# Moving the turned copy, the stores, the square sums and the weight preparation within a hand-ordered seven-product kernel

## Chip, cores, metric

One core of one Trainium2 chip. The metric is the device time of one execution in microseconds; lower is better.

## What is computed

A trunk of one layer over 2048 tokens of width 1024, all in float32:

```python
h = _rmsnorm(x, norm_w[layer])
proj = h @ w_in[layer]                       # split among four branches
y_a = _conv_mixer(a_h, a_b, a_c, a_z, ...)   # causal depthwise convolution, gated
y_b = _gla_mixer(g_q, g_k, g_v, g_lr, g_z, ...)   # gated linear attention, state per chunk of 64
y_c = _pool_mixer(p_u, p_z, ...)             # causal window means of 2, 4, 8, 16
y_d = _ssd_mixer(s_xbc, s_dt, s_z, ...)      # state space branch, state per chunk of 64
mix = jnp.concatenate([y_a, y_b, y_c, y_d], axis=-1)
x = x + mix @ w_out[layer]
return _rmsnorm(x, final_norm_w)
```

## The kernel before

**Arithmetic.** Every large float32 product is made of three matmuls on rounded halves: `split` (lines 172 to 174) casts a tile to `hi` on ACT (ScalarE) and takes `lo = raw - hi` on DVE (VectorE). `mm12` (lines 235 to 241) is one product of a 128x512 weight tile and a 512x512 quarter of the activations: four k-slices times three matmuls, 12 matmuls of 128x512.

**Seven products.** A 2x2 block product is done with seven `mm12` instead of eight, by sums and differences of quarters. `first7` (line 245) makes a11 x b11 in an accumulator `a`. `pair7` (lines 251 to 280) makes the other six. In order on TensorE they are s2, a12, s1, s3, then, through `after`, the first product (a11) of the next pair, then a22 and s4. The pair opens with the turned copy b = -a, an ACT instruction from PSUM to PSUM (lines 253 to 255); s2 accumulates onto b. There are four accumulator banks (`ps_acc`): a, b, e, and the a of the next pair. After each product a consumer empties a bank: `cp2` after s2, `ev11` after a12, `cp3` and a subtraction of e after s3, `ev21` after a22, and a last subtraction `d12 = e - d12` after s4.

**Runs.** The text calls one such product with its consumer and the `tick()` behind it a run: a pair has seven ticks. `tick` (lines 190 to 198) takes one step of four generators (`chunks`, the recurrence over chunks; `prep_`, the weights of the next pair; `side`, activations of the next stage, twice) and then runs those entries of `queue` that `later(n, fn)` put off by n ticks.

**Weights.** `prep7` (lines 216 to 233) asks for four raw 128x512 tiles, loads them, and then gives one step a tick: split a11 with the three POOL (GpSimd) sums s1, s2 and s3; split a12; and so on to s4. Its first step, the loads, is taken by `next(prep_[0])` ahead of the pair. It is drained at the end of each pair. The pool `pw` has 18 such tiles.

**Fixed order.** `strict[0]` turns on an order written out by hand: each engine's instructions, and the DMA issues on SP (SyncE), are issued in the order in which the program's text made them (class `Ordered`, lines 60 to 79). An instruction that waits holds up everything behind it on its engine. It is on from the first pair of each segment.

**Stages.** The tokens come in two segments of 1024. A segment begins with token-major blocks whose order the compiler picks; then come ten pairs in the fixed order, `qk, B, xs, C, a_h, a_c, a_b, a_z, p_u, p_z` (line 41). The recurrence (`chunk_loop`, lines 450 to 514) starts in pair C and ends near a_b; its output runs through `gate_outputs` and `to_mix` to DRAM (`yd`). Pairs a_z and p_z write `yd` by `spill` (line 578). In the last two pairs of a segment `side` makes the next segment's activations or, in the second, the halves of w_out. Then come eight row pairs (lines 1091 to 1106), each two tiles of 128 rows of `yd` times w_out: `Rows` (lines 1052 to 1089) adds the residual x, `square` (line 1025) sums the squares on ACT, `emit` (line 1032) does the inverse root on DVE in small steps (`rsqrt`, line 154), scales two halves of a row tile and stores them (`out`). `load_rows` reads `yd`, `load_x` reads x.

**The fold.** In the first segment `fold_pu` (line 346) multiplies the pool branch's weights on TensorE and writes them to DRAM (`wd`), before the pairs begin.

Of the kernel before, what the change touches and what calls it, by code (L numbers as in the profile page):

```python
# [55 lines left out]
def tile_hybrid_trunk(ctx: ExitStack, tc: tile.TileContext, xtok, xT, wkv, wch, wpu, wz, wo, pw_, nw, par, gw, fnw, out):  # L56
# [150 lines left out]


# [7 lines left out]
    def prep7(load, w7):  # L216

        a11, a12, a21, a22 = [wt("wr", F32) for _ in range(4)]
        load(a11, a12, a21, a22)
        yield 1  # L220
        w7['a11'] = split_w(a11)
        s1 = wt("ws", F32)
        pool.tensor_add(s1, a21, a22)
        s2 = wt("ws", F32)
        pool.tensor_add(s2, s1, a11)
        pool.tensor_add(a21, a21, a11)
        yield 1
        w7['a12'] = split_w(a12)
        pool.tensor_add(a12, a12, s2)
        yield 1  # L230
        for n, r in (('s2', s2), ('s1', s1), ('s3', a21), ('a22', a22), ('s4', a12)):
            w7[n] = split_w(r)
            yield 1
# [11 lines left out]
    def first7(w7, H):  # L245

        a = acc()
        mm12(a, w7['a11'], H['b11'], True)
        ahead[0] = a

    def pair7(w7, H, ev11, ev21, d12, d22, cp2, cp3, done, after=None):

        a = ahead[0]
        b = acc()
        act.activation(b, a, AF.Copy, scale=-1.0)
# [17 lines left out]
        mm12(b, w7['a22'], H['t4'], False)  # L273
        ev21(b)
# [71 lines left out]
    def fold_pu(j):  # L346

        mix = gen("mix")[:, :P]
        sp.dma_start(mix, pw_[j])

        def fold(h):
            wu = gen("wu")[:, :512]
            sp.dma_start(wu, wpu[j][:, h * 512:(h + 1) * 512])
            tp = tr()
            for i in range(4):
                pe.matmul(tp[:, i * P:(i + 1) * P], lhsT=wu[:, i * P:(i + 1) * P], rhs=mix, start=True, stop=True)
            raw = gen("fw")[:, :512]
            act.copy(raw, tp)
            sp.dma_start(wd[j][:, h * 512:(h + 1) * 512], raw)
        later(2, lambda: fold(0))  # L360
        later(3, lambda: fold(1))
# [88 lines left out]
    def chunk_loop(kv, kt, q, aG, aD, bt, xs, wt_, cc, after):  # L450
# [53 lines left out]
        for tt in range(TT):  # L504
            if tt:
                outputs(tt - 1, st)
            yield 1
# [5 lines left out]
        yield 1  # L513
        outputs(TT - 1, st)

    def gate_outputs(s, f, kv, xs, rt):
# [38 lines left out]
        def to_mix(tt):  # L555
# [11 lines left out]
            sp.dma_start(yd[s * TT + tt, :, 2:4, :], y3[:, 0:2, :])  # L567
            sp.dma_start(yd[s * TT + tt, :, 6:8, :], y3[:, 2:4, :])
# [9 lines left out]
    def spill(s, f, blk, y):  # L578

        t0 = s * TT + f * 4  # L580
        sp.dma_start(yd[t0:t0 + 4, :, blk, :].rearrange("t p n -> p t n"), y.rearrange("p (t n) -> p t n", t=4))
# [315 lines left out]
    for s in range(NSEG):  # L897
# [42 lines left out]
        prep_[0] = prep7(load_pair(PAIRS[0]), w7)  # L940
# [11 lines left out]
        drain(prep_)  # L952
        std.clear()
# [37 lines left out]
        first7(w7, H)  # L991
        for n, name in enumerate(PAIRS):
            w_next, wk = {}, []
            if n + 1 < len(PAIRS):
                prep_[0] = prep7(load_pair(PAIRS[n + 1]), w_next)
            elif s + 1 < NSEG:
                prep_[0] = kv_gen(wk)
            else:
                prep_[0] = prep7(load_rows(0), w_next)
            if w_next is not None and not (n + 1 == len(PAIRS) and s + 1 < NSEG):  # L1000
                next(prep_[0])
# [11 lines left out]
            drain(prep_)  # L1013
            w7 = w_next
        drain(side)
        strict[0] = s + 1 == NSEG
# [15 lines left out]
    def emit(tt, r, sq):  # L1032
        rs = rsqrt(None, None, 1, v=sq[:, 3:4])
        for c in range(2):
            cs = slice(c * 512, (c + 1) * 512)
            vec.scalar_tensor_tensor(r[:, cs], r[:, cs], rs, fw[c], ALU.mult, ALU.mult)
            sp.dma_start(out[tt, :, cs], r[:, cs])
# [14 lines left out]
    class Rows:  # L1052
# [12 lines left out]
        def ev11(self, o):  # L1065
            vec.tensor_tensor(self.r[0][0], o, self.x[0][0], ALU.add)
            square(self.r[0][0], self.x[0][0], self.sq[0], 0)

        def ev21(self, o):
            vec.tensor_tensor(self.r[1][0], o, self.x[1][0], ALU.add)  # L1070
            square(self.r[1][0], self.x[1][0], self.sq[1], 1)
# [7 lines left out]
        def done(self, j):  # L1079
            if j == 0:  # L1080
                square(self.r[1][1], self.x[1][1], self.sq[1], 0)
            elif j == 1:
                later(2, lambda: emit(self.tt + 1, self.rows[1], self.sq[1]))
            else:
                square(self.r[0][1], self.x[0][1], self.sq[0], 1)
                if self.tt + 2 < NTT:
                    later(3, lambda: emit(self.tt, self.rows[0], self.sq[0]))
                else:
                    emit(self.tt, self.rows[0], self.sq[0])

    rows = Rows(0)
    for tt in range(0, NTT, 2):
        w_next = {}
        nxt = []
        if tt + 2 < NTT:
            prep_[0] = prep7(load_rows(tt + 2), w_next)
            next(prep_[0])
# [4 lines left out]
        drain(prep_)  # L1102
# [83 lines left out]
```

## Time and profile before

| | us |
|---|---|
| median of 2 runs | 1009.86 (1004.94 to 1014.78) |
| the profiled execution | 1012.62 |
| its span, first to last instruction | 1010.8 |
| mean granted TensorE clock | 0.909 |

Times in the trace are microseconds from the span's start. Busy PE time counts overlapping matmuls once. A number in square brackets behind an instruction is the time that its engine idled just before it, and what ended that idle time. Every instruction of the fixed order has line 76, the line of the wrapper, so instructions are told apart by their tiles: `wh` and `wl` are the halves of weights, `wr` raw weights, `ws` the sums, `hh` and `hl` the halves of activations, `acc` the accumulators, `r` rows of the result, `xk` rows of x.

### The profile page before, as it was taken

To read this page: it belongs to the slowest core of one execution; us is meant where nothing else is said; L and a number is where in the kernel's file an instruction comes from. 1 tells how busy PE (TensorE), PEld (TensorE's weight loads), DVE (VectorE), ACT (ScalarE), POOL (GpSimd) and SP (SyncE) were. 2 spreads that over 40 slices of the span, in tenths; PEclk is the share of its full clock that TensorE was granted. 3 is DMA by queue.
4 is the path that set the end of the run, shared out by engine and by line. 5 is a ranking of instruction groups with operands and counts; after the bars stand their busy time and mean duration, and the time that the engine had idled before them with its cause. 6 is when DMAs were issued, how large, how long until landed. Compare 5 with 4: busy or idle time off the path is not lost. (4 is left out here: it accounts for less than half of the span.)

```text
span 1010.8 us, 11513 instructions
## 1 busy us (share of the span) xinstructions
PE 824.1 (82%) x3944; PEld 656.8 (65%) x3944; DVE 679.4 (67%) x1252; ACT 402.9 (40%) x804; POOL 257.1 (25%) x206
## 2 busy tenths in 40 slices
PE   7996798888868978899988889598862877787775
PEld 5885676666646757887766667477751666576564
DVE  5779556675857689835257766867699456655665
ACT  6756544442335334453344523334533222222221
POOL 0018222143421122302221445122243222220120
PEclk7999799999979999899999989889986988988888
DMA  9416411111113441222211102112701433233321
GB/s 321 150 59 204 159 42 42 42 42 49 36 52 115 148 158 47 79 74 81 86 42 42 42 1 84 53 53 88 287 21 37 150 125 108 92 114 125 117 92 63
DMA packets 57579, 94.09 MB, mean 93 GB/s; under 512 B 5840, under 2 KB 20656, under 8 KB 57008
## 3 DMA queue, kind: packets, MB, share of 16 engines
q1 hardware_dynamic: 57520, 93.35, 28.0%
q8 instruction: 31, 0.51, 0.2%
q14 instruction: 28, 0.23, 0.1%
HBM read 71.31 MB, written 22.02 MB: 92 GB/s over the span
## 5 line engine op out<-in xcount | busy, mean ns | idle before, releaser
L76 PE MATMUL acc<-hl,wh 128*128 128x512 f32 x782 | 335.8, 429 | 118.9 <-ACT acc L76 76.7
L76 PE MATMUL acc<-hh,wl 128*128 128x512 f32 x784 | 324.5, 414 | 8.1 <-DVE wl L76 8.1
L76 PE MATMUL acc<-hh,wh 128*128 128x512 f32 x784 | 324.5, 414 | 0.0
L76 PEld LDWEIGHTS acc<-hl,wh 128*128 128x128 f32 x782 | 159.0, 203 | 168.7 <-ACT acc L76 84.5
L76 PEld LDWEIGHTS acc<-hh,wl 128*128 128x128 f32 x784 | 158.6, 202 | 45.2 <-DVE wl L76 8.5
L76 PEld LDWEIGHTS acc<-hh,wh 128*128 128x128 f32 x784 | 159.8, 204 | 31.7
L76 DVE TENSOR_TENSOR wl<-wr,wh 128x512 fp32r<-128x512 f32 (+1 forms) x136 | 102.9, 757 | 82.0 <-ACT wh L76 74.5
L76 POOL TENSOR_TENSOR ws<-wr,wr 128x512 f32<-128x512 f32 x24 | 33.9, 1411 | 372.9 <-PE acc L76 121.6
L76 ACT CAST wh<-wr 128x512 fp32r<-128x512 f32 (+1 forms) x138 | 82.7, 604 | 62.4 <-DMA wr<-yd 53.1
L71 PE MATMUL acc<-wl,hh 128*128 128x512 f32 (+1 forms) x224 | 80.7, 364 | 8.2 <-DVE wl L76 7.4
L71 PE MATMUL acc<-wh,hl 128*128 128x512 f32 (+1 forms) x224 | 79.0, 358 | 0.0
L76 DVE SCALAR_TENSOR_TENSOR t<-xin,prm,t 128x512 f32<-128x512 f32 x72 | 59.4, 825 | 28.8 <-ACT t L76 25.9
L71 PE MATMUL acc<-wh,hh 128*128 128x512 f32 (+1 forms) x224 | 74.0, 363 | 4.8 <-ACT wh L71 4.8
L76 ACT ACTIVATE xk<-r 128x512 f32<-128x512 f32 x32 | 20.2, 631 | 96.6 <-DVE r L76 96.6
L71 PEld LDWEIGHTS acc<-wl,hh 128*128 128x128 f32 x224 | 44.7, 200 | 14.8 <-DVE wl L76 8.2
L76 POOL TENSOR_TENSOR wr<-wr,ws 128x512 f32<-128x512 f32 x26 | 37.1, 1425 | 65.6 <-DVE wl L76 45.8
L76 DVE TENSOR_TENSOR wl<-ws,wh 128x512 fp32r<-128x512 f32 x52 | 44.6, 857 | 8.7 <-ACT wh L76 5.5
L71 PEld LDWEIGHTS acc<-wh,hh 128*128 128x128 f32 x224 | 41.9, 197 | 11.4 <-ACT wh L71 6.7
L71 PEld LDWEIGHTS acc<-wh,hl 128*128 128x128 f32 x224 | 44.6, 200 | 4.9
L71 DVE TENSOR_TENSOR hl<-xq,hh 128x1024 fp32r<-128x1024 f32 (+1 forms) x36 | 44.1, 1245 | 4.3 <-ACT hh L71 4.3
L71 POOL TENSOR_TENSOR xq<-xq,xq 128x1024 f32<-128x1024 f32 x8 | 25.9, 3256 | 70.8 <-DVE xq L71 41.4
L71 ACT CAST hh<-xq 128x1024 fp32r<-128x1024 f32 (+1 forms) x36 | 35.1, 996 | 16.8 <-DVE xq L71 16.7
(216 smaller groups left out, 1153.0 us busy)
## 6 DMA issues: line engine op xcount, KB each, us to landing
wr<-in_wch SPq DMA_DIRECT2D x72, 256.0 KB, 2.9
xk<-in_xtok SPq DMA_DIRECT2D x64, 256.0 KB, 5.2
wr<-yd SPq DMA_DIRECT2D x32, 256.0 KB, 4.0
out<-r SPq DMA_DIRECT2D x32, 256.0 KB, 2.1
xq<-in_xT SPq DMA_DIRECT2D x14, 512.0 KB, 6.4
wr<-in_wz SPq DMA_DIRECT2D x16, 256.0 KB, 2.7
szd<-z SPq DMA_DIRECT2D x16, 256.0 KB, 2.8
sz<-szd SPq DMA_DIRECT2D x16, 256.0 KB, 2.9
```

What stands on the lines that cost most here:

```text
L71: return f(*args, **kw)
L76: r = f(*args, **kw)
```

## The change

It keeps the fixed order, and edits what stands where in it.

1. **The turned copy** moves out of the start of `pair7` into `second7`, which is called inside the pair before, behind the a22 product and ahead of `ev21`. The first pair of a segment calls it straight after `first7`.
2. **Weight preparation.** `load7` issues the loads where the pair starts, as before; `prep7` then makes one quarter a tick, and is not drained at the end of a pair. Steps left over are chained in front of the next pair's. The first pair of a segment waits one tick more (`n = 1`), so a11 of the next pair is split in tick 2 of a pair where it was tick 1, and s4 in tick 1 of the pair that uses it. s4 is summed into the tile of s2, after the split of s2, where it was summed into a12.
3. **Stores.** `store` puts a DMA issue off by one tick: the `y` and `yd` stores and the `out` stores of `emit`.
4. **Square sums** of the row pairs are put off by one tick, which puts them behind that tick's preparation step; the last `emit` as well.
5. **The recurrence** gives its two `yield`s after `advance`, so `outputs` of one step comes two ticks after `advance`, with `update` of the next step right behind it in the same tick. It needs 17 ticks where it needed 18.
6. **The fold** loads both halves of `wu` at once where `fold_pu` is called, and multiplies a tick later. The queue is emptied before the fixed order begins.

```diff
--- before.py
+++ after.py
@@ -205,19 +205,27 @@
         for _ in g or ():
             pass
-    def prep7(load, w7):
-        a11, a12, a21, a22 = [wt("wr", F32) for _ in range(4)]
-        load(a11, a12, a21, a22)
-        yield 1
+    def store(dst, src):
+        later(1, lambda: sp.dma_start(dst, src))
+    def load7(load):
+        raw = [wt("wr", F32) for _ in range(4)]
+        load(*raw)
+        return raw
+    def prep7(raw, w7, n=0):
+        a11, a12, a21, a22 = raw
+        for _ in range(n):
+            yield 1
         w7['a11'] = split_w(a11)
         s1 = wt("ws", F32)
         pool.tensor_add(s1, a21, a22)
@@ -226,9 +234,11 @@
         pool.tensor_add(a21, a21, a11)
         yield 1
         w7['a12'] = split_w(a12)
-        pool.tensor_add(a12, a12, s2)
         yield 1
-        for n, r in (('s2', s2), ('s1', s1), ('s3', a21), ('a22', a22), ('s4', a12)):
+        w7['s2'] = split_w(s2)
+        pool.tensor_add(s2, s2, a12)
+        yield 1
+        for n, r in (('s1', s1), ('s3', a21), ('a22', a22), ('s4', s2)):
             w7[n] = split_w(r)
             yield 1
@@ -246,13 +256,17 @@
         a = acc()
         mm12(a, w7['a11'], H['b11'], True)
-        ahead[0] = a
+        ahead[0] = [a, None]
+    def second7():
+        b = acc()
+        act.activation(b, ahead[0][0], AF.Copy, scale=-1.0)
+        ahead[0][1] = b
     def pair7(w7, H, ev11, ev21, d12, d22, cp2, cp3, done, after=None):
-        a = ahead[0]
-        b = acc()
-        act.activation(b, a, AF.Copy, scale=-1.0)
+        a, b = ahead[0]
         mm12(b, w7['s2'], H['t2'], False)
         cp2(d12, b)
         tick()
@@ -271,6 +285,8 @@
             after()
             tick()
         mm12(b, w7['a22'], H['t4'], False)
+        if after is not None:
+            second7()
         ev21(b)
         done(1)
         tick()
@@ -349,16 +365,19 @@
         sp.dma_start(mix, pw_[j])
         def fold(h):
-            wu = gen("wu")[:, :512]
-            sp.dma_start(wu, wpu[j][:, h * 512:(h + 1) * 512])
+            wu = wus[h]
             tp = tr()
             for i in range(4):
                 pe.matmul(tp[:, i * P:(i + 1) * P], lhsT=wu[:, i * P:(i + 1) * P], rhs=mix, start=True, stop=True)
             raw = gen("fw")[:, :512]
             act.copy(raw, tp)
             sp.dma_start(wd[j][:, h * 512:(h + 1) * 512], raw)
-        later(2, lambda: fold(0))
-        later(3, lambda: fold(1))
+        wus = []
+        for h in range(2):
+            wus.append(gen("wu")[:, :512])
+            sp.dma_start(wus[h], wpu[j][:, h * 512:(h + 1) * 512])
+        later(3, lambda: fold(0))
+        later(4, lambda: fold(1))
     last_exp = [None]
@@ -504,13 +523,12 @@
         for tt in range(TT):
             if tt:
                 outputs(tt - 1, st)
-            yield 1
             ups = update(tt, wx)
             if tt + 1 < TT:
                 wx = inputs(tt + 1)
             st = [advance(tt, i, ups[i]) for i in range(2)]
             yield 1
-        yield 1
+            yield 1
         outputs(TT - 1, st)
     def gate_outputs(s, f, kv, xs, rt):
@@ -564,8 +582,8 @@
                 act.activation(y[:, (2 + b) * P:(3 + b) * P], tp[:, (2 + b) * P:(3 + b) * P], AF.Copy,
                                scale=pcol('snw', b))
             y3 = y.rearrange("p (b n) -> p b n", b=4)
-            sp.dma_start(yd[s * TT + tt, :, 2:4, :], y3[:, 0:2, :])
-            sp.dma_start(yd[s * TT + tt, :, 6:8, :], y3[:, 2:4, :])
+            store(yd[s * TT + tt, :, 2:4, :], y3[:, 0:2, :])
+            store(yd[s * TT + tt, :, 6:8, :], y3[:, 2:4, :])
         later(3, scales_)
         for i, tt in enumerate(ts4):
@@ -578,7 +596,7 @@
     def spill(s, f, blk, y):
         t0 = s * TT + f * 4
-        sp.dma_start(yd[t0:t0 + 4, :, blk, :].rearrange("t p n -> p t n"), y.rearrange("p (t n) -> p t n", t=4))
+        store(yd[t0:t0 + 4, :, blk, :].rearrange("t p n -> p t n"), y.rearrange("p (t n) -> p t n", t=4))
     QS = ((0, 0), (0, 1), (1, 0), (1, 1))
@@ -937,7 +955,7 @@
             block_tok([std[0, 0], std[0, 1]], tt, wzt, o)
             spill_z(tt, o)
         w7 = {}
-        prep_[0] = prep7(load_pair(PAIRS[0]), w7)
+        prep_[0] = prep7(load7(load_pair(PAIRS[0])), w7)
         if s + 1 < NSEG:
             fold_pu(0)
             later(3, lambda: fold_pu(1))
@@ -950,6 +968,8 @@
             spill_z(4 + i, o[i])
         drain(side)
         drain(prep_)
+        while queue:
+            tick()
         std.clear()
         raws.clear()
         strict[0] = True
@@ -989,16 +1009,16 @@
             return a_pair(s, name)
         first7(w7, H)
+        second7()
         for n, name in enumerate(PAIRS):
             w_next, wk = {}, []
+            left = prep_[0] or ()
             if n + 1 < len(PAIRS):
-                prep_[0] = prep7(load_pair(PAIRS[n + 1]), w_next)
+                prep_[0] = chain(left, prep7(load7(load_pair(PAIRS[n + 1])), w_next, 0 if left else 1))
             elif s + 1 < NSEG:
-                prep_[0] = kv_gen(wk)
+                prep_[0] = chain(left, kv_gen(wk))
             else:
-                prep_[0] = prep7(load_rows(0), w_next)
-            if w_next is not None and not (n + 1 == len(PAIRS) and s + 1 < NSEG):
-                next(prep_[0])
+                prep_[0] = chain(left, prep7(load7(load_rows(0)), w_next))
             if name == 'C':
                 later(3, lambda: chunks.__setitem__(0, chunk_loop(kv, kt, q, aG, aD, bt, xs, wt_, cc, after_chunks)))
             if name == 'a_z':
@@ -1010,9 +1030,10 @@
             def after():
                 first7(w_next, H if n + 1 < len(PAIRS) else Hw)
             pair7(w7, H, *consumers(name), after=after if n + 1 < len(PAIRS) or s + 1 == NSEG else None)
-            drain(prep_)
             w7 = w_next
         drain(side)
+        if s + 1 < NSEG:
+            drain(prep_)
         strict[0] = s + 1 == NSEG
@@ -1034,7 +1055,7 @@
         for c in range(2):
             cs = slice(c * 512, (c + 1) * 512)
             vec.scalar_tensor_tensor(r[:, cs], r[:, cs], rs, fw[c], ALU.mult, ALU.mult)
-            sp.dma_start(out[tt, :, cs], r[:, cs])
+            store(out[tt, :, cs], r[:, cs])
     def load_x(tt):
         xk = []
@@ -1064,11 +1085,11 @@
         def ev11(self, o):
             vec.tensor_tensor(self.r[0][0], o, self.x[0][0], ALU.add)
-            square(self.r[0][0], self.x[0][0], self.sq[0], 0)
+            later(1, lambda: square(self.r[0][0], self.x[0][0], self.sq[0], 0))
         def ev21(self, o):
             vec.tensor_tensor(self.r[1][0], o, self.x[1][0], ALU.add)
-            square(self.r[1][0], self.x[1][0], self.sq[1], 1)
+            later(1, lambda: square(self.r[1][0], self.x[1][0], self.sq[1], 1))
         def cp2(self, d, o):
             vec.scalar_tensor_tensor(d, o, 1.0, self.x[0][1], ALU.mult, ALU.subtract)
@@ -1078,28 +1099,26 @@
         def done(self, j):
             if j == 0:
-                square(self.r[1][1], self.x[1][1], self.sq[1], 0)
+                later(1, lambda: square(self.r[1][1], self.x[1][1], self.sq[1], 0))
             elif j == 1:
                 later(2, lambda: emit(self.tt + 1, self.rows[1], self.sq[1]))
             else:
-                square(self.r[0][1], self.x[0][1], self.sq[0], 1)
+                later(1, lambda: square(self.r[0][1], self.x[0][1], self.sq[0], 1))
                 if self.tt + 2 < NTT:
                     later(3, lambda: emit(self.tt, self.rows[0], self.sq[0]))
                 else:
-                    emit(self.tt, self.rows[0], self.sq[0])
+                    later(1, lambda: emit(self.tt, self.rows[0], self.sq[0]))
     rows = Rows(0)
     for tt in range(0, NTT, 2):
         w_next = {}
         nxt = []
         if tt + 2 < NTT:
-            prep_[0] = prep7(load_rows(tt + 2), w_next)
-            next(prep_[0])
+            prep_[0] = chain(prep_[0] or (), prep7(load7(load_rows(tt + 2)), w_next))
             later(3, lambda: nxt.append(Rows(tt + 2)))
         rows.take()
         pair7(w7, H, rows.ev11, rows.ev21, rows.r[0][1], rows.r[1][1], rows.cp2, rows.cp3, rows.done,
               after=(lambda: first7(w_next, H)) if tt + 2 < NTT else None)
-        drain(prep_)
         w7 = w_next
         rows = nxt[0] if nxt else None
     while queue:
```

## Rows read from the trace of the kernel before

**Rows 1.** The page's busy time by engine.
```profile
PE 824.1 (82%) x3944; PEld 656.8 (65%) x3944; DVE 679.4 (67%) x1252; ACT 402.9 (40%) x804; POOL 257.1 (25%) x206
```

**Rows 2.** TensorE's waits: sum in us, how many, the longest.
```profile
PE acc L76 <- ACT acc L76: 76.7, 22, 8.7
PE acc L76 <- DVE r L76: 25.2, 8, 5.2
PE oy L76 <- POOL sb L76: 14.7, 12, 2.6
PE tr L71 <- DMA wu<-in_wpu: 12.4, 1, 12.4
```

**Rows 3.** Windows: length, busy PE, PEld, DVE, ACT, POOL, clock, DMA, GB/s.
```profile
115.70:377.90 262.20, 221.01 (x1133) 172.12 (x1134) 174.64 (x333) 104.02 (x210) 75.42 (x68) 0.93 0.23 73
...
480.40:710.70 230.30, 196.82 (x1024) 152.96 (x1024) 149.78 (x292) 94.26 (x190) 69.14 (x64) 0.93 0.18 55
710.70:782.20 71.50, 44.67 (x176) 35.60 (x176) 61.53 (x60) 29.43 (x46) 26.27 (x12) 0.81 0.32 113
...
807.60:980.50 172.90, 134.68 (x504) 105.82 (x504) 107.12 (x223) 43.05 (x96) 32.69 (x24) 0.88 0.33 110
980.50:1010.80 30.30, 18.58 (x72) 14.53 (x72) 16.12 (x51) 2.90 (x8) 0.00 (x0) 0.84 0.19 70
```

**Rows 4.** Groups by shape, the turned copy: busy us, mean ns of one, idle.
```profile
L76 ACT ACTIVATE acc<-acc 128x512 f32<-128x512 f32 x26 | 15.1, 582 | 0.0
```

**Rows 5.** Timeline, 863.5 to 866.6, end of one row pair: start, length, engine.
```profile
863.93 0.69 DVE L76 TENSOR_TENSOR r<-acc,r 128x512 f32<-128x512 f32 x1 [0.24 <-PE acc L76]
864.65 0.63 ACT L76 ACTIVATE xk<-r 128x512 f32<-128x512 f32 x1 [1.74 <-DVE r L76]
...
865.28 0.60 ACT L76 CAST wh<-wr 128x512 fp32r<-128x512 f32 x1
...
865.79 0.58 ACT L76 ACTIVATE acc<-acc 128x512 f32<-128x512 f32 x1
...
866.42 0.50 PE L76 MATMUL acc<-hl,wh 128*128 128x512 f32 x1 [2.53 <-ACT acc L76]
```

**Rows 6.** Timeline of TensorE in a row pair: matmuls at two spacings.
```profile
838.15 0.63 PE L76 MATMUL acc<-hh,wh 128*128 128x512 f32 x1
838.58 0.63 PE L76 MATMUL acc<-hh,wl 128*128 128x512 f32 x1
...
843.51 0.39 PE L76 MATMUL acc<-hh,wh 128*128 128x512 f32 x1
843.74 0.39 PE L76 MATMUL acc<-hh,wl 128*128 128x512 f32 x1
```

**Rows 7.** Timeline, SP's issues and ACT, start of the row pair at 866.
```profile
869.02 1.01 SPq L76 DMA_DIRECT2D out<-r  x2
870.13 1.85 SPq L76 DMA_DIRECT2D wr<-yd  x4
...
872.94 0.62 ACT L76 CAST wh<-wr 128x512 fp32r<-128x512 f32 x1 [6.57 <-DMA wr<-yd]
```

**Rows 8.** Timeline, DVE, POOL and PE within the row pair at 836.
```profile
837.24 0.22 DVE L76 SCALAR_TENSOR_TENSOR na<-ny,sq 128x1 f32<-128x1 f32 x1
...
847.86 1.70 POOL L76 TENSOR_TENSOR ws<-ws,wr 128x512 f32<-128x512 f32 x1
...
849.61 1.22 DVE L76 SCALAR_TENSOR_TENSOR ny<-na,ny 128x1 f32<-128x1 f32 x1
...
854.68 0.68 DVE L76 TENSOR_TENSOR r<-acc,xk 128x512 f32<-128x512 f32 x1
...
855.42 0.79 PE L76 MATMUL acc<-hl,wh 128*128 128x512 f32 x1 [3.14 <-DVE r L76]
```

**Rows 9.** Windows, pair a_c of the first segment.
```profile
250.90:292.10 41.20, 29.87 (x195) 21.43 (x193) 33.58 (x82) 14.09 (x31) 15.60 (x18) 0.91 0.21 65
```

## The prediction

> **What bounds the kernel now.** I read the page's busy times first. TensorE is busy for 824.1 of 1010.8 us and DVE for 679.4 [rows 1]: no engine is full, so the time is TensorE's work plus its waits, and the waits have to be named. The list of TensorE's waits names them: 76.7 us in 22 waits for the turned copy on ACT, 25.2 us for DVE in the row pairs, 14.7 us for the recurrence's POOL product, 12.4 us for one load of the fold [rows 2]. The copy itself takes 0.58 us [rows 4], so its 3.5 us a time are not its own length but its place in a queue. The windows then say where the waits lie: the idle time of PE is 41.2 us of 262.2 in the first segment's pairs, 33.5 of 230.3 in the second's up to p_u, 26.8 of 71.5 in the last two, and 38.2 of 172.9 in six row pairs [rows 3]. One more loss is in the clock column: 0.93 in the segments and 0.88 in the row pairs [rows 3]. Matmuls run 0.23 us apart at the full level of 2.4 GHz and 0.43 us apart for a while after a wait [rows 6], at 1.2 GHz. A pair's 84 matmuls take 84 x 0.23 = 19.3 us at the full level, one product 2.8 us.
>
> The end of a row pair shows what makes the copy late [rows 5]. The s4 product is done at 863.9; DVE subtracts (0.69), ACT squares that result (0.63), casts a quarter (0.60), and only then turns the accumulator (0.58); PE starts 2.53 us after it stopped. There are seven such rows in the row pairs, 17.7 us; 76.7 - 17.7 = 59.0 us fall on the 15 others, nearly all in the segments. The copy needs nothing but the first product, which was finished two products earlier.
>
> The second wait of a row pair: `out` stores go to SP ahead of the loads of `yd`, and SP waits with them for `emit` until 869.0; the loads go out at 870.1 and the cast of a11 waits 6.57 us until 872.9 [rows 7]. Everything behind that cast on ACT and its difference on DVE is late: cp3 starts at 854.7 in the pair at 836, and a22, which accumulates onto the same bank, waits 3.14 us for it [rows 8].
>
> **The change, part by part.** I sum against the profiled execution, 1012.62 us; the median of the runs is 2.8 us lower.
>
> *Turned copy.* Same instruction, same count, new place: it waits for a11 and runs while PE makes a22 and s4, 2 x 2.8 = 5.6 us of cover for 0.58. Behind it on ACT stands `ev21`, which waits for a22 anyway, so nobody is held up. It needs a bank while a', b and e live: that of the old a, which `ev11` emptied two runs before. If that cover were gone (ACT late by more than 5 us), the old wait of 2.5 to 3.5 us would be back. Bounds: 0 to 76.7 us gained. Not all, since a DVE that is behind shows up at the next place, where cp3 or the subtraction of e is late: in pair a_c DVE is busy 33.6 of 41.2 us [rows 9], against PE's 29.9, so its 8.7 us wait can shrink only to what DVE leaves. I take two thirds in the segments, 39 us of 59.
>
> *Recurrence.* `outputs` comes a tick later after `advance`, so POOL's product has a product's time more, 2.8 us against a longest wait of 2.6 [rows 2]. Bounds 0 to 14.7; I take 10. Against it: `outputs` now comes a tick sooner after pair C's own convolution, which may cost a wait of 2 to 3 us once a segment.
>
> *Clock.* At a mean of 0.93, 0.07 x 2 of 492.5 us is at the lower level [rows 3]; half of that, 34 us, is what it could give back, if all of it were busy. With most long waits gone I take 11. Segments together: 39 + 10 + 11 = 60, less 2 for the wait just named: 58 us.
>
> *Last two pairs of the second segment* (71.5 us): DVE is busy for 61.5 us [rows 3], making w_out's halves. No order of the queues removes that. Bounds 0 to 10; I take 5.
>
> *Row pairs.* They take 172.9 / 6 = 28.8 us each, with PE busy 22.4, DVE 17.9, ACT 7.2 [rows 3]. The change takes out the copy's wait; it lets the loads go ahead of the stores on SP (stores a tick later, two in tick 1 and two in tick 3, x loads between), and splits a11 in tick 2, 2.8 us later, so the loads have some 5 us more before anything needs them; it puts each square behind the cast of its tick, so ACT does not wait for DVE with a cast behind it. I followed the new order of DVE from the end of s4 (t = 0): subtraction, a22 split, `emit` of one row (3.1 us) to 4.6; cp2 to 5.3 (its bank is needed at 8.4); s4 split, ev11, a11 split to 7.5 (needed at 11.0); second `emit` to 10.6; a12 split, cp3 to 12.2 (needed at 13.8, when a11' ends); subtraction, s2, s1 to 14.3; then DVE waits for a22 and s4. It fits into 19.3 us, by 1.6 us at cp3. The small steps of `emit` are the risk: 0.22 us alone and 1.22 while POOL adds [rows 8], some 4 us a pair, which would eat that slack. So I take 21 us a pair, bounds 19.3 and 25: 6 x (28.8 - 21) = 47 us. The last pair (30.3 us with its tail) and the first lose 2 us each: 51 us in all.
>
> The Trainium skill has a rule against this: GPSIMD Engine Reference, section Specifications, says that GpSimd shares its SBUF interfaces with VectorE and contends with two-input DVE instructions. The trace agrees, 1.22 against 0.22 us [rows 8]. By that rule tick 2, where POOL's sums and `emit` now meet, costs the slack and the pair takes up to 25 us; it is the second case below.
>
> *The fold.* Loads of `wu` earlier: bounds 0 to 12.4 us [rows 2]. ACT and DVE finish the activations at about the same time, and the tiles are held longer, so I take 3. Its dearest loss is a wait of that same size for tiles that `wu` holds, 12 us.
>
> *Preparation.* Same instructions, one tick later. In the convolution pairs a11's split now stands behind two convolutions on DVE; by the same count it ends some 2 us after PE could use it in xs and C. That is within the third I left in. Stores by themselves cost nothing while SP is idle.
>
> Sum: 58 + 5 + 51 + 3 = 117; 1012.6 - 117 = 895.6, and 2.8 lower as a median: 893 us.
>
> **The rivals.**
>
> *Half of it* (25%). DVE becomes the bound: POOL meets `emit`, a22 waits for cp3 as it does now, a row pair takes 25 us, and in the segments late splits of a11 give back 20 us. Then 893 + 8 x 4 + 20 = 945. For it: DVE's 17.9 us a row pair leave 1.4 us of 19.3, and 33.6 in a_c [rows 3, 9]. Against it: DVE now spends much of a pair idle, waiting for casts that come late from DRAM [rows 7].
>
> *The copy's wait only moves* (6%). Four banks are all in use when the copy stands earlier; if the copy got b's bank and not that of a, it would wait for `ev21`, and s2 behind it. ACT had no idle time before the copy in any of the 26 [rows 4], so banks are not what it waits for now. Then the copy's gain goes and the rest, half of the row pairs and the recurrence, stays: 1010 - 25 - 10 = 975 to 1000.
>
> The Trainium skill would look there first: Perfetto Trace Analysis, section Optimization Strategy, says that a gap that repeats can mean too few buffers in SBUF or PSUM. The idle column of rows 4 speaks against it; no run here shows the new order yet.
>
> *Slower* (4%). On SP the x loads now stand ahead of late stores, and need `g` tiles that squares free later. If x of the next pair arrived after its cp2, each row pair would wait for a load: at the 6.57 us that the wait for `yd` is now [rows 7], plus the 3.14 behind it, each of 8 pairs loses 10 us, 80 in all, against 60 gained in the segments: 1030. It decides from the point where the loads land over 10 us late.
>
> **How the numbers follow.** The forecast has 65%, with a range of its own of 862 to 925: all of PE's idle time in the row pairs and segments gone at the lower end (another 31), half of the terms at the upper. Half of it has 25% (925 to 965), the moved wait 6%, slower 4%. To leave out no more than two in ten I take 862 to 955. What can be told from no change here is about 2%, 20 us. Faster by more than that: 65 + 25 + 2 = 0.92; within it 0.05; slower 0.03.
>
> **What would show it.** Right: the wait of PE for ACT's turned copy under 15 us; row pairs at 20 to 22 us with a clock near 1.0; loads of `yd` issued ahead of the stores; PE's wait for POOL under 5 us. Wrong: a22 still waiting for DVE in each row pair, a new row of PE waiting for a11's difference in xs and C, or x loads landing after cp2. What would make it wrong as a whole is DVE: if it is busy over 90% in the row pairs at more than 23 us a pair, the second case holds.

## The result, and the profile after

| | before | changed |
|---|---|---|
| median | 1009.86 us | 892.08 us (891.49 to 892.66) |
| the profiled execution | 1012.62 us | 891.49 us |
| its span | 1010.8 us | 889.4 us |
| mean granted TensorE clock | 0.909 | 0.936 |

The changed kernel takes 0.8834 of the time of before (95% interval 0.8647 to 0.902), 118 us less. The forecast was 893. The page's busy times, the answer to [rows 1]:

```profile
PE 778.3 (88%) x3944; PEld 631.4 (71%) x3944; DVE 667.8 (75%) x1252; ACT 400.8 (45%) x804; POOL 258.9 (29%) x206
```

The instruction counts are the same on every engine. TensorE's own busy time fell by 45.8 us with the same 3944 matmuls: that is the clock, whose granted mean rose from 0.909 to 0.936. The other 76 us of the 121.4 by which the span fell are idle time that went. The list of TensorE's waits (sum, how many, the longest), against [rows 2]:

```profile
PE acc L76 <- DVE wl L76: 18.3, 6, 9.2
PE acc L76 <- DVE r L76: 11.7, 2, 10.9
PE acc L76 <- ACT b L76: 11.1, 2, 5.6
...
PE acc L76 <- ACT wh L76: 7.1, 1, 7.1
...
PE oy L76 <- POOL sb L76: 2.9, 4, 1.0
```

The turned copy led the list of before with 76.7 us in 22 waits; it is gone from the head of this one. Of the six waits in the first row, one stood in the last pair before, too (8.1 us, now 9.2). The five others, 9.1 us together, are waits for the difference of a11 in the segments, which were not there before. In the row pairs DVE keeps PE waiting twice, where it was eight times, and one of the two is 10.9 us long. The stages, as windows (length, busy PE, PEld, DVE, ACT, POOL, clock, DMA, GB/s), against [rows 3]. The order is: the first segment's pairs up to p_u, the second's up to a_z, its last two pairs, the first row pair, the next six, the last:

```profile
118.20:350.00 231.80, 212.03 (x1132) 168.24 (x1133) 171.48 (x329) 103.20 (x209) 74.31 (x68) 0.95 0.24 78
452.10:654.60 202.50, 184.92 (x1028) 146.47 (x1029) 147.82 (x288) 91.53 (x187) 68.55 (x64) 0.97 0.19 62
654.60:714.60 60.00, 42.34 (x175) 33.65 (x173) 50.27 (x53) 26.70 (x44) 27.12 (x12) 0.83 0.38 136
714.60:747.20 32.60, 21.72 (x85) 17.46 (x86) 19.57 (x28) 10.42 (x20) 7.12 (x5) 0.84 0.47 153
747.20:861.70 114.50, 114.50 (x506) 94.57 (x505) 100.09 (x222) 42.18 (x96) 33.86 (x24) 1.00 0.48 159
861.70:889.40 27.70, 16.71 (x73) 13.23 (x71) 17.53 (x54) 4.13 (x11) 0.00 (x0) 0.87 0.20 76
```

In six row pairs PE is busy for all of the 114.5 us, at clock 1.00: 19.1 us a pair where it was 28.8. The end of such a pair, against [rows 5] and [rows 7] (timeline: start, length, engine):

```profile
782.95 1.76 SPq L76 DMA_DIRECT2D wr<-yd  x4
...
785.57 0.69 DVE L76 TENSOR_TENSOR r<-acc,r 128x512 f32<-128x512 f32 x1 [1.07 <-PE acc L76]
...
790.20 1.00 SPq L76 DMA_DIRECT2D out<-r  x2
791.25 1.87 SPq L76 DMA_DIRECT2D xk<-in_xtok  x4
```

The loads of `yd` leave 2.6 us before s4's subtraction; the stores of `out` come 7 us behind them. DVE is the one that waits at the end, 1.07 us for PE.

Two things got worse. The first row pair takes 32.6 us, and took 25.4. And the pairs begin at 118.2 us, and began at 115.7. Stage by stage the span's difference adds up so: start -2.5, segments 30.4 + 27.8 = 58.2, p_z with the second segment's start 0.5, last two pairs 11.5, first row pair -7.2, six row pairs 58.4, last 2.6, together 121.5, by rounding 0.1 more than the spans differ.

### The profile page after: what moved, and what is told of

It reads as the page before. It is cut to its first block, busy times and chain, and to the rows that moved or that the text cites. A ratio compares the mean times of both kernels' runs of the same rounds, so it can differ in the third digit from the quotient of the medians.

```text
span 889.4 us, 11454 instructions
## 1 busy us (share of the span) xinstructions
PE 778.3 (88%) x3944; PEld 631.4 (71%) x3944; DVE 667.8 (75%) x1252; ACT 400.8 (45%) x804; POOL 258.9 (29%) x206
## 5 line engine op out<-in xcount | busy, mean ns | idle before, releaser
L76 PE MATMUL acc<-hl,wh 128*128 128x512 f32 x782 | 320.2, 409 | 34.5 <-DVE r L76 11.7
L76 PE MATMUL acc<-hh,wl 128*128 128x512 f32 x784 | 315.0, 402 | 18.3 <-DVE wl L76 18.3
L76 PE MATMUL acc<-hh,wh 128*128 128x512 f32 x784 | 314.2, 401 | 0.0
L76 PEld LDWEIGHTS acc<-hh,wh 128*128 128x128 f32 x784 | 152.8, 195 | 30.3
L76 POOL TENSOR_TENSOR ws<-ws,wr 128x512 f32<-128x512 f32 x52 | 76.8, 1477 | 169.2 <-DVE wl L76 153.6
L76 DVE TENSOR_TENSOR wl<-wr,wh 128x512 fp32r<-128x512 f32 (+1 forms) x110 | 86.3, 787 | 12.9 <-ACT wh L76 12.5
L76 DVE TENSOR_TENSOR wl<-ws,wh 128x512 fp32r<-128x512 f32 x78 | 70.3, 909 | 18.0 <-ACT wh L76 17.9
L76 ACT CAST wh<-wr 128x512 fp32r<-128x512 f32 (+1 forms) x112 | 65.7, 598 | 16.1 <-DMA wr<-yd 9.5
L71 POOL TENSOR_TENSOR xq<-xq,xq 128x1024 f32<-128x1024 f32 x8 | 34.1, 4273 | 72.4 <-DVE xq L71 49.7
L76 ACT CAST wh<-ws 128x512 fp32r<-128x512 f32 x78 | 47.8, 621 | 12.7 <-POOL ws L76 11.0
```

What stands on the lines that cost most here:

```text
L71: return f(*args, **kw)
L76: r = f(*args, **kw)
```

## The experiments

Eleven more kernels ran, and the changed one again. Each ratio is to the kernel before, with its 95% interval. The kernel before took 1007.5 us in the runs beside the first eight and 1009.4 beside the last four, so the text gives times beside 892.2, the changed kernel run again among the first eight. Lengths of pairs and lines of traces are from the one profiled execution of each kernel, whose time can lie a few us off the median.

> The changed kernel as it is, for a base on the chip of these runs: 892 us, row pairs at 19.1 us.

It took 892.18 us, ratio 0.8861 (0.8829 to 0.8893).

### The turned copy: put back, and alone

One kernel is the changed one with the copy back at the start of the pair:

```diff
     def pair7(w7, H, ev11, ev21, d12, d22, cp2, cp3, done, after=None):
-        a, b = ahead[0]
+        a = ahead[0]
+        b = acc()
+        act.activation(b, a, AF.Copy, scale=-1.0)
```

and `second7` is left empty.

> The changed kernel with one part undone: the turned copy stands at the start of its pair again. Theory (the copy waited for its place in ACT's queue): TensorE waits at every pair start again, 2.1 to 2.5 us in the eight row pairs (DVE's subtraction 0.69, the square 0.63, the copy 0.58 and the gaps between them) and 2 to 3.5 us in most of the 18 pairs of the segments, some 60 us of waits and 10 us of clock: 945 to 965 us against 892. Rival (the copy's wait only showed that DVE was behind; loads, stores and preparation brought the gain): under 25 us lost, 900 to 915 us.

Measured: 949.94 us, 0.9428 (0.939 to 0.9466), a loss of 58, as expected. The first row of its list of TensorE's waits:

```profile
PE acc L76 <- ACT acc L76: 84.7, 22, 12.5
```

The other kernel is the one before with nothing but the copy moved.

> The kernel before with one part of the change alone: the turned copy in the pair ahead of its own. Theory: TensorE's wait for ACT's copy (76.7 us in 22) falls under 10 us; the row pairs keep their wait for DVE (25 us in all), since loads still stand behind stores. The gain is 45 to 75 us: 935 to 965 us. Rival (four banks all in use, the wait only moves): within 15 us of the kernel before, 995 to 1010 us, with a new row of TensorE waiting for DVE of some 60 us.

Measured: 972.74 us, 0.966 (0.9626 to 0.9694), a gain of 35, less than expected. The wait for the copy did fall, to 0.8 us. By the pairs' lengths, all of the gain is in the segments (40.4 us less) and in the last two pairs (2.9 less); the profiled execution of before, to which these lengths are compared, was itself 5 us longer than the median. The eight row pairs take 229.2 us, against 228.6 before. Its list of waits, first row, and a row pair's SP, ACT and PE:

```profile
PE acc L76 <- DVE r L76: 51.6, 9, 7.3
...
806.48 1.01 SPq L76 DMA_DIRECT2D out<-r  x2
807.59 1.84 SPq L76 DMA_DIRECT2D wr<-yd  x4
...
810.55 0.62 ACT L76 CAST wh<-wr 128x512 fp32r<-128x512 f32 x1 [7.21 <-DMA wr<-yd]
...
821.73 0.80 PE L76 MATMUL acc<-hl,wh 128*128 128x512 f32 x1 [6.79 <-DVE r L76]
```

In the row pairs the wait moved: the copy no longer waits, but the loads still stand behind the stores, the cast still waits 7.21 us, and the time comes back as 6.79 us before a22, which waits for cp3. So the copy is worth some 40 us in the segments in either direction (put back, it costs 18.9 + 20.8 there; 38 in all against the second profile of the changed kernel). In the row pairs it is worth nothing until the rest is done, and then 2 to 4 us a pair: put back, the pairs are 21.4 and 23.0 us long instead of 19.1.

### The stores

```diff
     def store(dst, src):
-        later(1, lambda: sp.dma_start(dst, src))
+        sp.dma_start(dst, src)
```

> The changed kernel with stores issued where they were, at once. Theory: two out stores stand ahead of the loads of yd again and SP waits for emit, which ends 4.6 us into the pair, so the loads land some 2 us later than now; with a11's split in tick 2 that still fits. 892 to 902 us, row pairs at 19.1 to 20.5 us. Rival (the stores were what held the row pairs at 28.8 us): row pairs at 23 us or more, over 920 us.

Measured: 931.58 us, 0.9257 (0.9219 to 0.9296), a loss of 39.4, so the rival's side. About 27 us of it are in the row pairs (21.3 to 24.6 us each), some 12 at p_z of the first segment (113.7 us to the next segment's first pair instead of 102.0). In a row pair, SP, ACT, POOL and DVE:

```profile
812.46 1.01 SPq L76 DMA_DIRECT2D out<-r  x2
813.57 1.84 SPq L76 DMA_DIRECT2D wr<-yd  x4
...
816.53 0.62 ACT L76 CAST wh<-wr 128x512 fp32r<-128x512 f32 x1 [5.82 <-DMA wr<-yd]
...
819.20 1.29 POOL L76 TENSOR_TENSOR ws<-wr,wr 128x512 f32<-128x512 f32 x1 [15.23 <-DMA wr<-yd]
...
820.54 3.54 DVE L76 SCALAR_TENSOR_TENSOR r<-r,ny,fw 128x512 f32<-128x512 f32 x2
```

The late load costs twice. ACT idles 5.82 us for it. And POOL's sums, late with it, now run beside the second `emit`, where two scalings take 3.54 us; without POOL beside them the pair takes 1.42. At p_z of the first segment, the loads of the next weights stand behind a `yd` store that waits for its data:

```profile
369.01 0.38 SPq L76 DMA_DIRECT2D yd<-pz  x1
369.49 2.41 SPq L76 DMA_DIRECT2D wr<-in_wkv  x5
...
372.52 0.83 PE L71 MATMUL acc<-wh,hh 128*128 128x276 f32 x2 [9.81 <-ACT wh L76]
```

In the changed kernel four of these loads are issued at 348.40, ahead of the stores.

Copy and stores together, and nothing else, put into the kernel before:

> The kernel before with two edits of the change: the turned copy in the pair before, and the stores a tick later. The preparation, the square sums, the recurrence and the fold stay as they were. Theory: in the row pairs the copy alone gained nothing because the casts that wait for late raw weights, behind the stores on SP, took its place; with both edits a row pair goes from 28.5 to 23 to 25 us and the whole from 973 to 930 to 945 us. Rival: the late casts come from the preparation's order or the squares, row pairs stay at 27 us or more, and the whole is over 955 us.

Measured: 939.71 us, 0.9301 (0.9247 to 0.9354), with row pairs of 23.6 us (one of 25.0). Both as expected: once the copy was out of the way, the loads behind the stores were a good half of what held the row pairs, 4.9 of the 9.4 us by which 28.5 is over 19.1. After the first row pair no cast waits for a load any more. The rest is DVE: PE still waits 1.4 us for cp2 and 2.6 for cp3 in such a pair.

### The square sums

```diff
-            later(1, lambda: square(self.r[0][0], self.x[0][0], self.sq[0], 0))
+            square(self.r[0][0], self.x[0][0], self.sq[0], 0)
```

and so for the other squares and the last `emit`.

> The changed kernel with the square sums (and the last emit) of the row pairs at once, ahead of the tick's preparation step. Theory: a square waits on ACT for DVE's result with the next cast behind it, and DVE's difference behind the cast: about 0.8 us at each of three places in a row pair, of which the slack at cp3 (1.6 us) takes part: row pairs at 19.1 to 20.5 us, 892 to 902 us. Rival (the squares were a main part of the row pairs' 28.8 us): over 21 us a pair, over 905 us.

Measured: 912.87 us, 0.9064 (0.9029 to 0.9099), a loss of 20.7, again the rival's side: row pairs of 22.0 to 22.9 us. In one pair PE waits 1.47 and 1.59 us for DVE's cp2 and cp3. DVE itself waits for ACT, where a square that waits for DVE's sum stands ahead of the cast that DVE needs next:

```profile
793.38 0.63 ACT L76 ACTIVATE xk<-r 128x512 f32<-128x512 f32 x1 [1.43 <-DVE r L76]
...
794.14 0.16 DVE L76 SCALAR_TENSOR_TENSOR sq<-sq 128x1 f32<-128x1 f32 x1 [0.79 <-ACT xk L76]
794.65 0.69 DVE L76 TENSOR_TENSOR wl<-wr,wh 128x512 fp32r<-128x512 f32 x1 [0.35 <-ACT wh L76]
```

There are four such pairs of waits in each row pair, 1.1 us each: 4.6 us of DVE's time. PE's two waits are 3.1 us together. Not all of them need come from the squares alone: the scalings of the first `emit` also take 3.46 us here, beside POOL, where they take 2.34 in the changed kernel.

### The preparation, the recurrence, the fold

The preparation as it was, a tick sooner and drained at the pair's end, with s4 summed into a12 again:

```diff
-            yield 1
-        w7['s2'] = split_w(s2)
-        pool.tensor_add(s2, s2, a12)
-        yield 1
-        for n, r in (('s1', s1), ('s3', a21), ('a22', a22), ('s4', s2)):
+        pool.tensor_add(a12, a12, s2)
+        yield 1
+        for n, r in (('s2', s2), ('s1', s1), ('s3', a21), ('a22', a22), ('s4', a12)):
```

> The changed kernel with the preparation of before: a11's split in tick 1, all seven quarters made and the generator drained within the pair, s4 summed into a12. Theory: the later tick is what gives the loads of yd their time; with a11 in tick 1 its cast waits on ACT for a load that was issued less than 4 us before, and ev11 and the square stand behind it, so 1 to 2 us come back in each row pair and as much in some segment pairs: 900 to 915 us. Rival (preparation costs nothing either way, the order of SP is what counts): within 5 us of 892.

Measured: 914.28 us, 0.9074 (0.9043 to 0.9105), a loss of 22: 8.5 in the segments, 8.5 in the eight row pairs (six of them at 20.6 to 21.2 us), most of the rest in the second segment's p_z. The time is in the expected range, but the row pairs do not show the expected mechanism. After the first of them no cast waits for a load of `yd`: a11's runs in tick 1 right behind the square (the first line). PE waits for cp3, and DVE has small steps before it that are slow beside POOL's sums, one of them the second line:

```profile
802.60 0.61 ACT L76 CAST wh<-wr 128x512 fp32r<-128x512 f32 x1
...
806.54 1.24 DVE L76 SCALAR_TENSOR_TENSOR sq<-sq 128x1 f32<-128x1 f32 x1
...
816.06 0.50 PE L76 MATMUL acc<-hl,wh 128*128 128x512 f32 x1 [1.26 <-DVE r L76]
```

It lies beside a POOL sum (806.15 to 807.77) and takes 1.24 us, and 0.15 in the changed kernel, where other instructions meet POOL. So in the row pairs the later tick seems to be worth what it keeps apart on DVE, POOL and ACT, and not time for the loads; no run singles that out. The new preparation is not free of cost: pairs xs and C take 53.1 us together with the old one, and 57.1 and 55.5 with the new one.

The `yield`s of the recurrence as before:

> The changed kernel with the recurrence's two yields where they were, outputs one tick after advance. Theory: TensorE waits for POOL's product again, 7 us a segment, the most in pairs a_h and a_c: 900 to 908 us. Rival (with the copy early TensorE reaches outputs no sooner than POOL is done, or DVE sets these pairs): within 4 us of the changed kernel.

Measured: 906.34 us, 0.9008 (0.8976 to 0.9041), a loss of 14. In the segments' pairs it is 10.0 us, and PE's wait for POOL comes back (the other 4 us are the distance of this profiled execution, 902.64 us, from the median):

```profile
PE oy L76 <- POOL sb L76: 13.7, 10, 4.2
```

The fold as before, each half of `wu` loaded in the tick of its own product, and the queue not emptied:

> The changed kernel with the fold of before: wu loaded where it is used, a tick sooner, and the queue not emptied ahead of the fixed order. The pairs begin at 118.2 us now and at 115.7 before, so the fold's edit seems to have cost 2.5 us. Theory (TensorE's wait for wu only turned into one for the z copies behind ACT's squares): 888 to 893 us. Rival (the start differs by chance of the compiler's order, or the earlier loads do help): 895 us or more.

Measured: 897.1 us (896.24 to 901.23), 0.8919 (0.8886 to 0.8951), some 5 us behind the changed kernel, whose runs beside it ranged from 889.74 to 894.32. The pairs begin at 124.3 us. PE's wait for `wu` is 20.6 us in this kernel and 2.4 in the changed one. So in the changed kernel the earlier loads seem to gain, although its pairs begin later than those of before. It is not shown beyond doubt: the intervals of the two ratios overlap, and the compiler orders this stretch anew in each kernel.

### How much DVE has left in a row pair

Two or six small products more in each `emit`, two emits a pair:

```diff
     def emit(tt, r, sq):
+        scr = prm[:, PC['id']:PC['id'] + 256]
+        for _ in range(2):
+            vec.tensor_tensor(scr, scr, scr, ALU.mult)
```

> The changed kernel with two products of 128x256 more on DVE in every emit, of 0.4 us each by the adds of that size, so 1.7 us more DVE work in each row pair (16.7 busy of 19.1). They only square the identity matrix onto itself. Theory: a row pair has 1.6 to 2.4 us of slack on DVE, so each pair grows by 0 to 1 us: 892 to 900 us. Rival (DVE already sets the pace of the row pairs): every microsecond put in comes out, 8 pairs x 1.7 = 13 us, over 903 us.

> The changed kernel with six products of 128x256 more on DVE in every emit, some 5 us more DVE work in each row pair. Theory: the slack of 1.6 to 2.4 us is used up and the rest is paid, 2.6 to 4 us in each of 8 pairs: 912 to 925 us, row pairs of 21.7 to 23 us. Rival (DVE has ample slack, its idle time being spread as it is needed): under 900 us.

Measured: 907.05 us, 0.8991 (0.8949 to 0.9033), with row pairs of 21.7 us; and 943.08 us, 0.9331 (0.929 to 0.9372), with row pairs of 25.2 us (one of 26.8). The first is on the rival's side. The second missed on the far side: it is slower than the 912 to 925 expected, where the rival was faster. With 4 x 0.42 = 1.7 us put in, a pair grows by 2.6; with 12 x 0.515 = 6.2 put in, by 6.1. The first grows by more than was put in because the shift brought two small steps of DVE beside POOL's sums, 1.24 us each; DVE's busy time in the pair went from 16.69 to 19.27 us, by as much as the pair grew. There is no slack where the work was put, though DVE still idles elsewhere. One pair of the first of the two kernels, PE and DVE:

```profile
790.00 0.69 DVE L76 TENSOR_TENSOR r<-acc,r 128x512 f32<-128x512 f32 x1 [1.03 <-PE acc L76]
...
799.11 0.47 PE L76 MATMUL acc<-hl,wh 128*128 128x512 f32 x1 [0.98 <-DVE r L76]
```

DVE waits 1.03 us for PE at the end of s4, and PE waits 0.98 us for DVE at cp2: idle time at one end of the pair cannot pay for work at the other. In the changed kernel itself the margin at cp3 is the gap between these two lines, 779.65 to 779.88:

```profile
778.96 0.69 DVE L76 TENSOR_TENSOR r<-acc,xk 128x512 f32<-128x512 f32 x1
...
779.88 0.40 PE L76 MATMUL acc<-hl,wh 128*128 128x512 f32 x1
```

It is 0.23 us at most.

### The first row pair

SP's queue around it, and PE's wait, in the changed kernel:

```profile
710.77 15.00 SPq L76 DMA_DIRECT2D yd<-pz  x3
725.83 0.98 SPq L76 DMA_DIRECT2D fw<-in_fnw  x2
726.86 1.87 SPq L76 DMA_DIRECT2D xk<-in_xtok  x4
728.89 2.68 SPq L76 DMA_DIRECT2D wr<-yd  x4
...
733.98 0.77 PE L76 MATMUL acc<-hl,wh 128*128 128x512 f32 x1 [10.85 <-DVE r L76]
```

DVE's cp2 needs x, and x is issued behind three stores of the last pair that wait for their data until 725.8. One more kernel issues the loads of x and of the final weights inside the last pair:

```diff
+            if name == 'p_z' and s + 1 == NSEG:
+                later(5, lambda: rows0.append(Rows(0)))
+                later(6, load_fw)
```

> The changed kernel, but the four loads of x of the first row pair are issued five ticks into the last pair of the second segment, and the two loads of the final weights six ticks into it, instead of behind that pair's stores. Theory: the first row pair is long (32.5 us against 19.1 for those after it) because its x loads stand on SP behind three stores of the last pair that wait for their data; with the loads ahead, PE's wait of 10.85 us at the first row pair's second product falls under 4 us, that pair takes 22 to 27 us, and the whole 882 to 888 us. Rival: the first row pair is long because of the raw weights or of DVE, and stays over 30 us; the whole is then 890 to 894 us.

Measured: 884.99 us (881.52 to 886.25), 0.8752 (0.8708 to 0.8795), 7 us ahead of the changed kernel (by the ratios to the kernel before, 11) and the fastest of all. The first row pair takes 26.5 us:

```profile
712.06 2.21 SPq L76 DMA_DIRECT2D xk<-in_xtok  x4
...
721.35 5.30 SPq L76 DMA_DIRECT2D yd<-pz  x2
...
728.26 0.77 PE L76 MATMUL acc<-hl,wh 128*128 128x512 f32 x1 [4.33 <-DVE r L76]
```

The wait that is left, 4.33 us, is a little over the 4 expected.

## Why the prediction was right, point by point

**The sum held, and by luck better than its terms.** Forecast and measured gain, in us:

| term | forecast | measured |
|---|---|---|
| segments | 58 | 58.2 |
| last two pairs of the second | 5 | 11.5 |
| six row pairs | 47 | 58.4 |
| first and last row pair | 4 | -4.6 |
| fold and start | 3 | -2.5 |
| p_z with the second segment's start | 0 | 0.5 |

So 117 were forecast and 121.5 found, with misses of 11.4 and 6.5 on one side and 8.6 and 5.5 on the other. That the median came within 1 us of the forecast is luck; that it came into the range is not: the waits that it named in the segments and the row pairs are the ones that went.

**Segments.** In the prediction's own terms, waits were to give 39 + 10 - 2 = 47 us and the clock 11. Of the 58.2 us, 37.3 are idle time and 20.9 shorter busy time of the same matmuls; the granted clock rose from 0.93 to 0.95 and 0.97. Two misses of 10 us cancelled, so the 58 was luck too. The single edits, taken back one at a time, say the same in another way: copy 39.7, recurrence 10.0, preparation 8.5, waits and clock together (38, 8 and 7 against the second profile of the changed kernel). The preparation stood at nothing in the sum.

**The floor of DVE in a_c showed in the next pair.** I held DVE's 33.6 busy us in a_c [rows 9] against the copy's gain. Pair a_c now takes 28.8 us, with DVE busy 24.2 (windows of a_c and a_b):

```profile
240.70:269.50 28.80, 27.37 (x205) 20.56 (x203) 24.16 (x60) 9.37 (x21) 13.06 (x15) 1.00 0.20 65
269.50:302.30 32.80, 25.27 (x103) 19.97 (x101) 28.06 (x71) 14.08 (x34) 5.82 (x4) 0.84 0.21 60
```

82 DVE instructions stood in a_c and 60 do now: work slid into the next pair, and a_b, the second line, grew from 28.7 to 32.8 us. There a DVE that is behind does show up at the next place, as I had said. PE waits 5.58 us for a copy on ACT, which stands behind an activation that waits for DVE:

```profile
283.57 0.79 PE L76 MATMUL acc<-hl,wh 128*128 128x512 f32 x1 [5.58 <-ACT b L76]
```

Together the two pairs went from 69.9 to 61.6 us, where the wait for the copy alone had been 8.7.

**Row pairs.** I took 21 us for fear of `emit`'s small steps, with 19.3 as the bound below; 19.1 came, since the matmuls run 0.227 us apart and I had rounded up. The step that failed is where POOL would meet DVE. The small steps do run at 0.22 us in both emits. POOL's sums meet the big scalings of the first `emit` instead, and three splits (DVE in one row pair):

```profile
768.05 0.22 DVE L76 SCALAR_TENSOR_TENSOR na<-ny,sq 128x1 f32<-128x1 f32 x1
...
769.40 2.34 DVE L76 SCALAR_TENSOR_TENSOR r<-r,ny,fw 128x512 f32<-128x512 f32 x2
...
772.33 1.30 DVE L76 TENSOR_TENSOR wl<-ws,wh 128x512 fp32r<-128x512 f32 x1
...
776.97 1.42 DVE L76 SCALAR_TENSOR_TENSOR r<-r,ny,fw 128x512 f32<-128x512 f32 x2
```

Up to cp3 that costs 0.92 us for the two scalings, some 0.6 for the split shown and 0.5 for another: 2.0 us, not 4. (A third split, behind cp3, loses 0.5 more.) cp3 ended 13.2 us after s4, where my walk had 12.2, and a22 could start at 13.4, where it had 13.8: the 1.6 us that the walk left came out as 0.23, and PE did not wait. The trace agrees with the rule of the Trainium skill (GPSIMD Engine Reference, Specifications) that GpSimd contends with VectorE instructions that have two SBUF inputs: 2.34 us beside a sum against 1.42. My price for it was loosely read: the 1.22 us of [rows 8] is the step `ny`, which takes 0.16 alone and not the 0.22 of `na`, and the POOL sum beside it is the next one, from 849.52, and not the one shown.

**Half of it (25%)** did not come, but it was closer than its time of 945 makes it look: 1.7 us more work on DVE takes a row pair to 21.7, and 6.2 to 25.2, its own figure. What I wrote against it, that DVE spends much of the pair idle, was right as far as it went: DVE idled 65.8 us in six row pairs before and 14.4 after. But the 2.4 us a pair that are left lie where nothing can use them.

**The copy's wait only moves (6%)** was right for the row pairs in a form that I hadn't described: not through a bank, but through SP's queue, as the kernel with the copy alone shows. There are four banks in all these kernels. The Trainium skill (Perfetto Trace Analysis, Optimization Strategy) names too few buffers as one possible cause of a gap that repeats. The traces show another: the wait for the copy fell from 76.7 to 0.8 us when nothing but its place changed.

**"Stores by themselves cost nothing while SP is idle"** was wrong. SP is idle, but its order isn't free: a store that waits for its data holds the loads behind it, and that is worth 39.4 us in the changed kernel, some 12 of them at p_z of the first segment, which the prediction never looked at. In the row pairs I did count it, in the loads that go ahead.

**Slower (4%)** named x loads that land after cp2, and that did come, in one row pair of eight, where it costs 7 us. The cause was another than I gave: not tiles that squares free late, but stores of the last pair that stand ahead of the loads on SP.

**The later tick** was to give the loads some 5 us more. The new preparation as a whole is worth 22 us, but with the old one no cast waits for a load in the row pairs after the first. Once the stores are out of the way, the loads are early enough for either tick.

**Last two pairs.** I put the 59.0 us outside the row pairs "nearly all in the segments". One of those 15 waits, 0.1 us short of the longest, stood at the end of the last pair of the kernel before:

```profile
782.22 0.80 PE L76 MATMUL acc<-hl,wh 128*128 128x512 f32 x1 [8.57 <-ACT acc L76]
```

So the segments held 50.4, and an order of the queues could gain here too. But the 11.5 are no gain of that size. DVE was busy 58.6 us in p_z and the first row pair before and 58.8 after (39.2 + 19.6), but 9 us of it moved from the one to the other. Together the two stages went from 75.2 to 73.0 us.

**The fold.** The wait for `wu`, 12.4 us [rows 2], is now this (PE):

```profile
100.60 2.04 PE L71 MATMUL tr<-mix,wu 128*128 128x128 f32 x8 [2.38 <-DMA wu<-in_wpu]
112.02 0.79 PE L73 MATMUL acc<-hl,wh 128*128 128x512 f32 x1 [9.37 <-ACT z L71]
```

It became a wait for ACT, as I allowed for with 3 of 12.4 us. That the pairs begin 2.5 us later all the same, and 8.6 later with the old fold (124.3), is not explained: the kernels with the other parts taken back one at a time begin at 118.2 to 120.3, and no run singled the cause out.

**The smaller signs.** One sign of being wrong did show: the a11 difference is late, in C by 1.33 us in both segments, in a_b by 1.9 and 2.5 and in one p_u by 2.0, and I had looked for it in xs and C alone. xs and C are some 2 to 4 us longer a segment for the preparation, as I had it (2 in each). `outputs` a tick sooner costs 1.0 and 1.2 us in C and not 2 to 3. PE's wait for POOL is 2.9 us (forecast under 5), the waits for the turned copy are well under 15, the clock of the row pairs is 1.00. The upper end of the forecast's own range, 925, was not "half of the terms", as I wrote: half of 117 would be 951. All parts taken back singly lose 58 + 39.4 + 22 + 20.7 + 14 + 5 = 159 us, where the whole gained 118. The parts overlap: in the row pairs any one of four edits missing costs 1.5 to 5.5 us a pair, and only all of them together bring the 19.1.

## What to carry to other kernels

In a fixed order, look at each in-order queue for an instruction that waits, and at what stands behind it that could go: here a copy behind a square and a cast behind a square, both on ACT, and loads behind stores on SP were the same fault. Mending one of them shows the next (the copy alone gained nothing in the row pairs), so cost such edits together and by the stage, and test them by taking one at a time out of the whole. When the tight stage runs without a gap, ask how near the next bound is: here 0.23 us, at one place of the pair, while the same engine idled 1.07 us at another.

## What the runs showed of the hardware that I had not expected

POOL's adds slow DVE's large instructions by a size that depends on how they overlap: two 128x512 scalings took 1.42 us alone, 2.34 beside one add and 3.54 beside two. Where one of DVE's two inputs is in PSUM the add costs nothing: cp2 and ev11 (`r<-acc,xk`) took 0.68 us at 771.73 and 773.55, each beside an add, as they do alone. The mean of all 32 such scalings went from 748 to 924 ns with the change, while nothing was added to them; the mean of the small step `na` fell from 443 to 220 ns. The granted clock stayed at 1.00 for six row pairs on end once PE had no gap. In the kernel with six products more, a wait of 2.65 us that ended at 781.67 was followed by eight matmuls 0.43 us apart (granted clock 0.52 from there to 785.11), and another of 2.65 that ended at 806.88 by matmuls 0.23 apart (granted clock 1.00 over as long): the first cost some 1.6 us more than its own length.
